# Where the stored queries and keys of two attention dilations are rotated: a GpSimd stream through DRAM, or VectorE one unit ahead

## The chip, the cores and the metric

The kernel runs on one core of one Trainium2 chip. A core has TensorE (PE, with a weight-load path PEld), VectorE (DVE), ScalarE (ACT), GpSimd (POOL) and SyncE (SP), each with an instruction queue of its own that is worked off in order. The metric is the device time of one execution in microseconds (us); less is better. In the profile `L126` is line 126 of the kernel, `psu<-t2h,w` is what an instruction writes and reads, and `[1.58 <-ACT u L365]` behind an instruction is the time its engine stood idle before it and what ended that.

## The reference

A decoder trunk of two layers over 1024 tokens of width 1024. Layer 0 mixes tokens with a gated delta rule and short convolutions, layer 1 with four HGRN2 heads (a gated recurrence) and with sliding-window attention in three dilations; each is followed by a dense feed-forward network. The change is in layer 1:

```python
SWA_PATTERNS = ((128, 1), (512, 4), (2048, 16))
...
def mixer_cd(h, w_in, lower_bound, norm_g, w_out):
    hq, hf, hi, hg, sq, sk, sv = split_cols(h @ w_in, CD_SPLITS)
...
    f_gate = lb + (1.0 - lb) * jax.nn.sigmoid(hf)
    o_c = hgrn2_recurrence(...)
...
    sq = rope(sq.reshape(b, t, n_pat, SWA_HEADS, SWA_DH), pos)
    sk = rope(sk.reshape(b, t, n_pat, SWA_HEADS, SWA_DH), pos)
...
def rope(x, pos):
    x1, x2 = xf[..., :half], xf[..., half:]
    return jnp.concatenate([x1 * cos - x2 * sin, x1 * sin + x2 * cos], axis=-1)
```

`rope` is the rotation: every head's 128 rows are two halves of 64; the result is the row times a cosine, plus the row of the other half times a signed sine. With the exchanged copy `x` of a tile `c` (its halves swapped) it is three element-wise instructions: `x*sin`, `c*cos`, and their sum.

## The kernel before

All large products are made in three passes of a reduced format (high by high, high by low, low by high), so `L126`, `L127`, `L128` are the three matmuls of one product, and `L102` and `L103` split a weight into its two parts on ACT and VectorE.

**The projection stage** (class `Pairs`) makes the queries and keys of dilation patterns 0 (dilation 1) and 2 (dilation 16), and the HGRN gates, with a product scheme that shares partial products between pairs of columns. For each pair, `pair` (L906) calls steps `p1` to `p7`. `p6` (L362) adds a product onto an accumulator `x[f]` and copies it to SBUF on ACT (L365, tile `u`); `p7` goes on adding onto the same accumulator, so PE must wait for that copy. Between `p6` and `p7` PE has the products of `p5`. `step` (L836) works off one piece of the forget gate of an HGRN head (`forget`, L816): among them a reciprocal on VectorE (L828), an instruction that makes `kk` from it (L830), and an activation on ACT that waits for it (L832). In this stage PE, VectorE, ACT, GpSimd, and from the pair loop on SyncE too, run in the order in which the code is written. The queries and keys go to DRAM unrotated, as `qk[p, h]` (L804).

**The mixer** (`mixer_cd`) then runs, on PE in the written order and on the other engines in the order that a scheduler picks by priority and readiness: the value projections of a dilation pattern (`swa_v`, whose tiles `sw` ACT copies at L1884 and SyncE writes to `scr_v` at L1885), the projection and VectorE rotation of pattern 1's queries and keys (`swa_qk`, L1914 and L1915), the HGRN recurrence (its level products at L1713 and L1715, its attention at L1791 and L1811, its norm at L1818 to L1825, of which L1821 is on GpSimd), and the attention itself. The attention has 12 units (`Attend`): pattern 1 heads 0 to 3, pattern 2 heads 0 to 3, pattern 0 heads 0 to 3. A unit has 4 steps of scores (PE L2014 and others from `k` and `q`, reduced by VectorE at L2020 or L2039), with flips and output products one and two steps later, and outputs that go out by SyncE as `scr_o<-ol` (L2090 and L2097).

The generator `local` gives one score step each time it is asked, and holds one unit ahead of the current one: `prepare` builds it, which issues its loads. A counter (`tick`) asks three generators as the projections go on: `local` at 0.7 and later 1.0 per unit of cost, the HGRN chain at 0.7, and the rotations at 0.5.

**The rotation stream** (`turns`) is that third generator. It has 32 items (two patterns, four heads, queries and keys, two halves). For each it loads a half `tc` (L1930) and its exchanged copy `tx` (L1931, L1932), rotates on GpSimd (L1943 for pattern 0, L1947 for pattern 2, the sum at L1948), and stores to DRAM as `fin` (L1950). A unit of patterns 2 and 0 reads `fin` when it is built:

```python
while not all((p, h, i, half) in turned for i in range(2) for half in range(NH)):
    next(turner)
self.q, self.k = tl("q", (2, HT), 2), tl("k", (2, HT), 2)
dma(self.k, final[p, h][1])
```

SyncE issues every one of these transfers, together with the weights (`raw`), the recurrence's loads (`f`, `kk`, `q` from `bkq`) and the value tiles.

## Time and profile before

| | before |
|---|---|
| median of 3 runs | 2625.44 us (2623.76 to 2626.53) |
| the profiled execution, its time | 2629.71 us |
| its span, first to last instruction | 2627.9 us |
| mean granted TensorE clock | 0.991 |
| DMA | 464.42 MB, mean 177 GB/s |

The rotation stream's part of GpSimd, from the groups of instructions between 1400 and 1600 us (line, engine, operation, tiles, shapes, count, then busy us, mean ns of one, and the engine's idle time before them with what ended it):

```profile
L1948 POOL TENSOR_TENSOR tc<-tc,tx 128x512 f32<-128x512 f32 x32 | 43.4, 1356 | 2.5
L1947 POOL TENSOR_TENSOR tc<-tc,turn 128x512 f32<-128x512 f32 x16 | 24.6, 1536 | 26.0 <-DMA tc<-qk 26.0
L1943 POOL TENSOR_TENSOR tc<-tc,turn 128x512 f32<-128x512 f32 x16 | 21.4, 1335 | 16.6 <-DMA tc<-qk 16.6
```

And its transfers on SyncE's queue (tiles, kind, count, size of one, median us from issue to landing):

```profile
tc<-qk SPq DMA_DIRECT2D x32, 256.0 KB, 3.8
fin<-tc SPq DMA_DIRECT2D x32, 256.0 KB, 3.8
k<-fin SPq DMA_DIRECT2D x8, 512.0 KB, 3.7
```

The stream is over by 1600 us: all 32 sums lie in that window, for units whose scores on PE begin at 1724.5 (pattern 2, L2032) and 1796.8 us (pattern 0).

### The profile page before, as it was taken

The numbers are of one execution on the slowest core, as the hardware profiler recorded it, in microseconds if no ns is written. First come the engines' busy times: TensorE is split into PE (matmuls) and PEld (weight loads), VectorE is DVE, ScalarE is ACT, GpSimd is POOL, SyncE is SP. The second block draws the span as 40 slices with busy tenths as digits, with TensorE's granted clock in tenths as the row PEclk, the third lists the DMA queues.
The fourth block names the chain that finished last, engine by engine and source line by source line (L and its number), as shares of the span: only waits on it lengthen the run. The fifth ranks groups of instructions, "written<-read, shape, count | busy, mean of one in ns | idle before, by whom it ended". The sixth has DMA issues, their size and how long they took to land.

```text
span 2627.9 us, 37803 instructions
## 1 busy us (share of the span) xinstructions
PE 2564.8 (98%) x14179; PEld 2138.1 (81%) x14179; DVE 1656.1 (63%) x2718; ACT 1032.6 (39%) x1855; POOL 643.5 (24%) x536
## 2 busy tenths in 40 slices
PE   8999999999999999999999879999999999999998
PEld 6888888888888888888788768878788888888887
DVE  7887776585656565566664675444667665566553
ACT  5432123343333344434343444455544333334442
POOL 1110111333333300133324762000024433331001
PEclk9999999999999999999999989999999999999999
DMA  4424346425556688533336874466662445668753
GB/s 141 137 98 163 108 150 216 145 85 168 188 185 220 206 300 285 182 112 124 117 111 222 258 212 138 113 169 214 191 237 74 164 166 197 206 204 288 268 186 119
DMA packets 291559, 464.42 MB, mean 177 GB/s; under 512 B 50704, under 2 KB 141616, under 8 KB 291248
## 3 DMA queue, kind: packets, MB, share of 16 engines
q1 hardware_dynamic: 291376, 462.01, 53.9%
q8 instruction: 111, 1.82, 0.3%
q14 instruction: 72, 0.59, 0.1%
HBM read 315.55 MB, written 146.36 MB: 176 GB/s over the span
## 4 chain that ended last, share of the span: by engine, by line
PE 79%; DVE 9%; DMA 4%; issue 3%; ACT 2%; POOL 2%; SPq 1%; POOLq 0%; DVEq 0%; ACTq 0%
PE psu L126 15%; PE psu L128 15%; PE psu L127 15%; PE psg L126 5%; PE psg L128 5%; PE psg L127 5%; PE psm L127 4%; PE psm L128 4%; PE psm L126 4%; DMA tc<-qk 1%; DVE fc L828 1%; DMA cm<-scr_o 1%; PE psm L2072 1%; DVE h L223 1%; DMA raw<-in_dram 1%
## 5 line engine op out<-in xcount | busy, mean ns | idle before, releaser
L103 DVE TENSOR_TENSOR w<-raw,w 128x1024 fp32r<-128x1024 f32 (+1 forms) x319 | 388.3, 1220 | 160.9 <-ACT w L102 160.4
L102 ACT CAST w<-raw 128x1024 fp32r<-128x1024 f32 (+1 forms) x319 | 306.8, 963 | 281.0 <-PE psu L128 134.7
L126 PE MATMUL psu<-hnh,w 128*128 128x512 f32 x888 | 356.8, 402 | 8.0 <-ACT w L102 8.0
L127 PE MATMUL psu<-hnl,w 128*128 128x512 f32 x888 | 349.1, 393 | 0.2 <-DVE hnl L2250 0.2
L128 PE MATMUL psu<-hnh,w 128*128 128x512 f32 x888 | 349.1, 393 | 0.0
L126 PEld LDWEIGHTS psu<-hnh,w 128*128 128x128 f32 x888 | 168.5, 190 | 42.2 <-ACT w L102 8.4
L128 PEld LDWEIGHTS psu<-hnh,w 128*128 128x128 f32 x888 | 168.3, 190 | 36.4 <-DVE w L103 0.8
L127 PEld LDWEIGHTS psu<-hnl,w 128*128 128x128 f32 x888 | 168.6, 190 | 34.2 <-DVE hnl L2250 0.8
L187 POOL TENSOR_TENSOR acc<-acc,sq 128x512 f32<-128x512 f32 x48 | 69.7, 1452 | 511.4 <-ACT sq L183 507.3
L302 POOL TENSOR_TENSOR ws<-raw 128x512 f32<-128x512 f32 x50 | 73.6, 1473 | 422.2 <-DMA raw<-in_dram 295.2
L103 DVE TENSOR_TENSOR w<-ws,w 128x1024 fp32r<-128x1024 f32 x47 | 61.6, 1311 | 116.0 <-ACT w L102 116.0
L103 DVE TENSOR_TENSOR hidq<-hr,hidq 128x1024 fp32r<-128x1024 f32 x72 | 82.2, 1143 | 73.8 <-ACT hidq L102 73.4
L102 ACT CAST hidq<-hr 128x1024 fp32r<-128x1024 f32 x72 | 70.2, 979 | 99.5 <-DMA hr<-ts 60.8
L126 PE MATMUL psm<-hidq,w 128*128 128x512 f32 (+1 forms) x275 | 106.1, 386 | 0.0
L128 PE MATMUL psm<-hidq,w 128*128 128x512 f32 (+1 forms) x275 | 105.9, 385 | 0.0
L127 PE MATMUL psm<-hidq,w 128*128 128x512 f32 (+1 forms) x275 | 105.9, 385 | 0.0
L126 PE MATMUL psu<-t3h,w 128*128 128x512 f32 x224 | 87.7, 392 | 5.6 <-ACT u L365 5.6
L393 POOL TENSOR_TENSOR hid<-hid,c 128x512 f32<-128x512 f32 x44 | 61.5, 1397 | 125.2 <-ACT hid L392 124.8
L308 POOL TENSOR_TENSOR raw<-raw,ws 128x512 f32<-128x512 f32 x47 | 61.3, 1304 | 121.0 <-DVE w L103 119.8
L126 PE MATMUL psu<-t4h,w 128*128 128x512 f32 x224 | 87.6, 391 | 0.6 <-ACT c L372 0.5
L127 PE MATMUL psu<-t3l,w 128*128 128x512 f32 x224 | 87.3, 390 | 0.0
L127 PE MATMUL psu<-t4l,w 128*128 128x512 f32 x224 | 87.3, 390 | 0.0
(489 smaller groups left out, 6655.2 us busy)
## 6 DMA issues: line engine op xcount, KB each, us to landing
raw<-in_dram SPq DMA_DIRECT2D x227, 512.0 KB, 3.7
sd<-in_dram SPq DMA_DIRECT2D x44, 512.0 KB, 3.7
hid<-hid SPq DMA_DIRECT2D x88, 256.0 KB, 3.1
sd<-sd SPq DMA_DIRECT2D x44, 512.0 KB, 3.3
hr<-ts SPq DMA_DIRECT2D x40, 512.0 KB, 4.9
raw<-sd SPq DMA_DIRECT2D x40, 512.0 KB, 4.0
hd<-h SPq DMA_DIRECT2D x48, 256.0 KB, 3.4
h<-hd SPq DMA_DIRECT2D x48, 256.0 KB, 5.8
```

Source lines behind the costliest of these rows:

```text
L102: S.copy(hi, src)
L103: eng.tensor_tensor(lo, src, hi.bitcast(F32), op=SUB)
L126: T.matmul(o, lh, rh, start=first and i == 0, stop=False, **kw)
L127: T.matmul(o, lh, rl, start=False, stop=False, **kw)
L128: T.matmul(o, ll, rh, start=False, stop=last and i == n - 1, **kw)
L187: (eng or G).tensor_tensor(a, a, q, op=ADD)
L223: V.scalar_tensor_tensor(h, h, vec[:, row + k:row + k + 1], pb, op0=MULT, op1=MULT)
L302: G.tensor_tensor(s[:, HT:], b[:, :HT], b[:, HT:], op=ADD)
L308: G.tensor_tensor(a[:, HT:], a[:, HT:], s[:, :HT], op=SUB)
L393: G.tensor_tensor(h, h, self.c22.pop(f), op=MULT)
L828: V.reciprocal(c, c)
L2072: T.matmul(po[:, jj * P:(jj + 1) * P], pt[:, z.start + i * P:z.start + (i + 1) * P], self.vp[:, j - m + 1 + i, :], start=i == 0, stop=i == ...
```

## The change

In `pair`, `p6` now stands ahead of the `step()` that stood ahead of it. The stream, its third counter, the tiles `tc` and `tx`, and the DRAM tensors `fin` are gone. A unit of patterns 2 and 0 loads its `k` and `q` unrotated from `qk`, and their exchanged copies as `rs` (two tiles of 512 KB, two buffers), when it is built; it leaves a list `todo` of four parts, each three VectorE instructions (two products and a sum, 128x512). `local` does two of the parts before the third and two before the fourth score step of the unit ahead of it, and what is left when the unit becomes the current one. The table of sines and cosines becomes one tile `turn` with room for the larger table; pattern 0's (1 MB) is loaded over the other's. Pattern 2's queries are rotated in place in their strided order.

```diff
@@ -931,8 +931,8 @@
             self.part_a(n, an)
             self.sums_late(an, bn, s)
             self.row1(f - 1, b22)
+            self.p6(f, t2)
             self.step()
-            self.p6(f, t2)
             self.p5(f, t1, psg())
             self.part_b(n, s)
             self.part_c(n, bn)
@@ -1893,13 +1893,22 @@
                     for tt, o in zip(tts, os_):
                         put(tt, o)
 
-            turn12 = tl("turn12", (2, 320))
-            dma(turn12, c_rope[:, :, T_LEN:])
-            final = {(p, h): dr.tile([2, P, 2, HT], F32, name=f"fin{p}{h}") for p in (2, 0) for h in range(4)}
+            table = {}
+
+            def turn(p):
+
+                if (p == 0) not in table:
+                    table.clear()
+                    t = table[p == 0] = tl("turn", (2, T_LEN))
+                    if p:
+                        dma(t[:, :, 0:320], c_rope[:, :, T_LEN:])
+                    else:
+                        dma(t, c_rope[:, :, 0:T_LEN])
+                return table[p == 0]
 
             def swa_qk(h, tick):
 
-                w = wload(("cd", 20 + h), ("cd", 32 + h))
+                w, turns = wload(("cd", 20 + h), ("cd", 32 + h)), turn(1)
                 qk = [tl("q", (2, HT), 2), tl("k", (2, HT), 2)]
                 for half in range(NH):
                     for i, z in enumerate(qk):
@@ -1911,44 +1920,10 @@
                         S.copy(x[64:128], o[0:64])
                         o3, x3 = (y.rearrange("p (i r) -> p i r", r=4) for y in (o, x))
                         for y, t in ((x3, 1), (o3, 0)):
-                            V.tensor_tensor(y, y, turn12[:, t, half * P:(half + 1) * P, None].to_broadcast([P, P, 4]), op=MULT)
+                            V.tensor_tensor(y, y, turns[:, t, half * P:(half + 1) * P, None].to_broadcast([P, P, 4]), op=MULT)
                         V.tensor_tensor(z[:, half].rearrange("p (r i) -> p i r", r=4), o3, x3, op=ADD)
                         tick(1)
                 return qk
-
-            def turns():
-
-                items = [(2, h, i, half) for h in range(4) for i in range(2) for half in range(NH)]
-                items += [(0, h, i, half) for half in range(NH) for h in range(4) for i in range(2)]
-                held, table, out = {}, {}, []
-
-                def ask_c(n):
-                    if n < len(items):
-                        p, h, i, half = items[n]
-                        held[n] = c, x = tl("tc", bufs=2), tl("tx", bufs=2)
-                        src = pairs.qk[p, h][i, :, half]
-                        dma(c, src)
-                        dma(x[0:64], src[64:128])
-                        dma(x[64:128], src[0:64])
-                ask_c(0)
-                for n, (p, h, i, half) in enumerate(items):
-                    if p == 0 and half not in table:
-                        table[half] = tl("turn0", (2, HT))
-                        dma(table[half], c_rope[:, :, half * HT:(half + 1) * HT])
-                        yield
-                    c, x = held.pop(n)
-                    ask_c(n + 1)
-                    for y, t in ((x, 1), (c, 0)):
-                        if p == 0:
-                            G.tensor_tensor(y, y, table[half][:, t], op=MULT)
-                        else:
-                            y3 = y.rearrange("p (r i) -> p r i", r=16)
-                            at = 256 + half * 32
-                            G.tensor_tensor(y3, y3, turn12[:, t, None, at:at + 32].to_broadcast([P, 16, 32]), op=MULT)
-                    G.tensor_tensor(c, c, x, op=ADD)
-                    yield
-                    dma(final[p, h][i, :, half], c)
-                    turned.add((p, h, i, half))
 
             def values(h, p):
                 vp = tl("vp", (8, P), 2)
@@ -1972,23 +1947,45 @@
 
                 def __init__(self, h, p, qk):
                     self.h, self.p = h, p
+                    self.todo = []
                     if p == 1:
                         self.q, self.k = qk
                     else:
-                        while not all((p, h, i, half) in turned for i in range(2) for half in range(NH)):
-                            next(turner)
-                        self.q, self.k = tl("q", (2, HT), 2), tl("k", (2, HT), 2)
-                        dma(self.k, final[p, h][1])
-                        if p == 2:
-                            c = self.q.rearrange("p b t -> p (b t)").rearrange("p (s b i) -> p b s i", s=16, b=2)
-                            for b in range(2):
-                                dma(c[:, b], final[p, h][0, :, b].rearrange("p (s i) -> p s i", s=16))
-                        else:
-                            dma(self.q, final[p, h][0])
+                        self.load(turn(p), pairs.qk[p, h])
                     self.vp = values(h, p)
                     self.tiles = [1 + ((p == 0 and j > 0) or (p == 1 and j % 2 == 1)) for j in range(8)]
                     self.sc, self.pt, self.po = {}, {}, None
                     self.st = tl("stat", (8, 2), 3)
+
+                def load(self, turns, src):
+
+                    self.k, self.q = tl("k", (2, HT), 2), tl("q", (2, HT), 2)
+
+                    def streams(ap):
+                        return ap.rearrange("p (s i) -> p s i", s=16) if self.p else ap
+
+                    def part(c, x, b):
+                        for y, t in ((x, 1), (c, 0)):
+                            if self.p:
+                                t = turns[:, t, None, 256 + b * 32:288 + b * 32].to_broadcast([P, 16, 32])
+                            else:
+                                t = turns[:, t, b * HT:(b + 1) * HT]
+                            V.tensor_tensor(y, y, t, op=MULT)
+                        V.tensor_tensor(c, c, x, op=ADD)
+
+                    for i, t in ((1, self.k), (0, self.q)):
+                        if self.p and i == 0:
+                            c4 = t.rearrange("p b t -> p (b t)").rearrange("p (s b i) -> p b s i", s=16, b=2)
+                            cs = [c4[:, b] for b in range(2)]
+                            for b in range(2):
+                                dma(cs[b], src[i, :, b].rearrange("p (s i) -> p s i", s=16))
+                        else:
+                            cs = [streams(t[:, b]) for b in range(2)]
+                            dma(t, src[i])
+                        x = tl("rs", (2, HT), 2)
+                        dma(x[0:64], src[i, 64:128])
+                        dma(x[64:128], src[i, 0:64])
+                        self.todo += [lambda c=cs[b], y=streams(x[:, b]), b=b: part(c, y, b) for b in range(2)]
 
                 def blocks(self, n):
 
@@ -2151,7 +2148,7 @@
                 end[1]()
 
             lead = {}, {}, {}, (6, 7)
-            ready, late, diag, turned, holding, combined = [], [], [], set(), [0], [0]
+            ready, late, diag, holding, combined = [], [], [], [0], [0]
 
             def local():
 
@@ -2164,7 +2161,13 @@
                 while True:
                     nxt = None
                     prepare()
+                    if now and ahead and now[1] > 1:
+                        for turn_part in ahead[0].todo[:2]:
+                            turn_part()
+                        del ahead[0].todo[:2]
                     if not now and ahead:
+                        for turn_part in ahead[0].todo:
+                            turn_part()
                         now += [ahead.pop(), 0]
                         prepare()
                     holding[0] = len(ahead) + bool(now)
@@ -2185,13 +2188,13 @@
                     yield
 
             busy = [False]
-            hg_chain, loc, turner = chain(), local(), turns()
-            works = (loc, hg_chain, turner)
-            due, rate = [0.0] * 3, [0.0, 0.7, 0.5]
+            hg_chain, loc = chain(), local()
+            works = (loc, hg_chain)
+            due, rate = [0.0] * 2, [0.0, 0.7]
 
             def tick(cost):
 
-                for i in range(3):
+                for i in range(2):
                     due[i] += cost * rate[i]
                 while max(due) >= 1:
                     for i, work in enumerate(works):
```

**SyncE while the value tiles of pattern 2 are projected.** The rows of an engine's order give line, operation, and tiles (`scr_v` value tiles to DRAM, `raw` a weight, `kk` and `q<-bkq` inputs of the recurrence, `vt` its values). SyncE before, at the start of this stretch:

```order
L1931 DMA tx<-qk_9313 64x512
L1932 DMA tx<-qk_9313 64x512
L115 DMA raw<-in_dram 128x1024
L1930 DMA tc<-qk_9313 128x512
L1885 DMA scr_v_11037<-sw 128x512
L1950 DMA fin_11054<-tc 128x512
L1885 DMA scr_v_11037<-sw 128x512
L1931 DMA tx<-qk_9314 64x512
L1932 DMA tx<-qk_9314 64x512
L1885 DMA scr_v_11037<-sw 128x512
L1930 DMA tc<-qk_9314 128x512
L1950 DMA fin_11054<-tc 128x512
```

SyncE of the changed kernel at the same place:

```order
L115 DMA raw<-in_dram 128x1024 x2
L1762 DMA vt<-scr_h 128x4x128
L1694 DMA kk<-bkq_9318 128x512
L1694 DMA q<-bkq_9318 128x512
L1885 DMA scr_v_11037<-sw 128x512 x4
L1762 DMA vt<-scr_h 128x4x128
```

The value tiles, which stood between loads and stores of the rotation, now follow one another.

**ACT in `pair`.** In the order of ACT before, the activation of the forget gate (L832) and then the copy of `p6` (`u`); `w` are weight casts and `d` is another accumulator's copy:

```order
L832 ACTIVATE fc<-fc,lb,omlb 128x512
L338 COPY gt<-psu 128x512
L857 COPY d<-psu 128x32x16
L102 CAST w<-raw 128x1024
L832 ACTIVATE fc<-fc,lb,omlb 128x512
L365 COPY u_10138<-psu 128x512
L102 CAST w<-ws 128x1024
```

and of the change:

```order
L832 ACTIVATE fc<-fc,lb,omlb 128x512
L338 COPY gt<-psu 128x512
L857 COPY d<-psu 128x32x16
L102 CAST w<-raw 128x1024
L365 COPY u_10132<-psu 128x512
L832 ACTIVATE fc<-fc,lb,omlb 128x512
L102 CAST w<-ws 128x1024
```

The copy has moved ahead of the second activation.

**SyncE at the handover from pattern 2 to pattern 0.** Before: `k` and `q` of the first unit of pattern 0 from `fin`, among output tiles `scr_o<-ol` and value tiles:

```order
L2097 DMA scr_o<-ol 64x4x130 x2
L1981 DMA k<-fin_11057 128x1024
L1987 DMA q<-fin_11057 128x1024
L2097 DMA scr_o<-ol 64x4x130 x2
L115 DMA raw<-in_dram 128x1024 x3
L2097 DMA scr_o<-ol 64x4x130 x2
L1885 DMA scr_v_11036<-sw 128x512 x2
```

The change, at the same place (the first two `rs` are the exchanged halves of the keys, the others of the queries; line 2094 was line 2097):

```order
L115 DMA raw<-in_dram 128x1024
L1984 DMA k<-qk_9309 128x1024
L1986 DMA rs<-qk_9309 64x1024
L1987 DMA rs<-qk_9309 64x1024
L2094 DMA scr_o<-ol 64x4x130 x2
L1885 DMA scr_v_11036<-sw 128x512
L1984 DMA q<-qk_9309 128x1024
L1885 DMA scr_v_11036<-sw 128x512
L1986 DMA rs<-qk_9309 64x1024
L2094 DMA scr_o<-ol 64x4x130 x2
L1885 DMA scr_v_11036<-sw 128x512
L1987 DMA rs<-qk_9309 64x1024
```

The queries and their exchanged halves now stand behind two output tiles and three value tiles of the running unit. VectorE at that place in the change (`q`, `rs` as above, `k` the next unit's keys; L2017 is the score reduction of pattern 0, which was L2020; `ol<-stat` belongs to the outputs, `ss` and `e` to the recurrence's norm):

```order
L1973 TENSOR_TENSOR q<-q,turn 128x512 x2
L2089 COPY ol<-stat 64x4x2
L2091 COPY ol<-stat 64x2x2 x2
L1819 TENSOR_SCALAR ss<-ss 128x4
L1825 TENSOR_TENSOR e_15325<-psg,rr 128x512
L1973 TENSOR_TENSOR rs<-rs,turn 128x512 x2
L1974 TENSOR_TENSOR q<-q,rs 128x512 x2
L1973 TENSOR_TENSOR k<-k,turn 128x512 x2
L2017 ISA sc,stat<-psm,cf 128x128
```

The rows of L1973 and L1974 are new here. The sums of the queries (L1974) now stand just ahead of the first score reduction of pattern 0, with two products of the next unit's keys between.

## The prediction

> **What bounds the kernel now.** I read the busy times first, then the chain that ended last, the stretches of the stage that the change touches, and the waits of TensorE (PE) in them.
>
> ```profile
> PE 2564.8 (98%) x14179; PEld 2138.1 (81%) x14179; DVE 1656.1 (63%) x2718; ACT 1032.6 (39%) x1855; POOL 643.5 (24%) x536
> ...
> PE 79%; DVE 9%; DMA 4%; issue 3%; ACT 2%; POOL 2%; SPq 1%; POOLq 0%; DVEq 0%; ACTq 0%
> ```
>
> PE is busy for 98% of the span and its instruction order is the same in both kernels, row for row. So a gain can only come out of PE's idle time and out of the time at a lowered clock, and a loss is a new PE wait. The profiled execution took 2629.7 us, with a span of 2627.9 us; the median of the three runs is 2625.4 us, 4.3 below it. I sum against the 2629.7 and put the sum on the median. The next view has stretches of layer 1's mixer; its columns are the stretch, its length, then busy time (and count) of PE, PE's weight loads, VectorE (DVE), ScalarE (ACT), GpSimd (POOL), then the granted clock, the DMA share and GB/s.
>
> ```profile
> 1400.00:1500.00 100.00, 90.80 (x900) 78.59 (x900) 53.04 (x81) 36.58 (x95) 69.38 (x51) 0.95 0.76 241
> 1500.00:1600.00 100.00, 85.18 (x923) 75.92 (x922) 71.14 (x127) 45.02 (x125) 66.53 (x49) 0.93 0.72 217
> 1600.00:1700.00 100.00, 97.38 (x903) 82.09 (x902) 58.08 (x153) 49.02 (x137) 2.09 (x2) 0.98 0.41 109
> ```
>
> POOL works for two thirds of the first two stretches, and these hold the PE's idle time: 9.2 + 14.8 = 24.0 us, against 2.6 us in the third, where the rotations are done. The PE's waits between 1400 and 1600 (engine, line, what it waited for: total us, times, longest) give the same 24:
>
> ```profile
> PE psm L2014 <- DVE k L1915: 12.2, 1, 12.2
> PE psg L1811 <- ACT attn L1791: 7.4, 2, 6.8
> PE psm L2061 <- ACT sc L2021: 2.2, 2, 2.0
> PE psg L1814 <- DVE st L1807: 1.8, 2, 1.4
> PE psm L2014 <- DVE stat L2020: 0.5, 1, 0.5
> ```
>
> No row names GpSimd, so I follow each wait one step back.
>
> ```profile
> 1448.73 0.58 ACT L1884 COPY sw<-psu 128x512 f32<-128x512 f32 x1 [9.09 <-DMA scr_v<-sw]
> ...
> 1558.22 0.69 DVE L1825 TENSOR_TENSOR e<-psg,rr 128x512 f32<-128x512 f32 x1 [3.47 <-POOL rr L1821]
> ...
> SPq L1950 <- POOL tc L1948: 44.5, 24, 4.6
> ...
> L1713 DVE TENSOR_TENSOR kd<-kd,dd 128x256 f32<-128x256 f32 x18 | 19.3, 1073 | 0.9 <-ACT e L1818 0.5
> ...
> L1713 DVE TENSOR_TENSOR kd<-kd,dd 128x256 f32<-128x256 f32 x18 | 7.6, 424 | 1.7 <-ACT m L1710 1.1
> ```
>
> Three ways lead back to the stream. SyncE issues every transfer in order and stood 44.5 us behind rotated tiles (third row); so ACT, ahead of the attention tile, stood 9.09 us for a value tile's write (first row). DVE stood 3.47 us for `rr`, which is queued on GpSimd behind the rotations (second row). And the same VectorE instruction takes 1073 ns between 1410 and 1560 but 424 ns between 1600 and 1720 (last two rows): beside the GpSimd stream VectorE is 2.5 times as slow. The Trainium skill, "SBUF — State Buffer", section "Who interferes with whom", says that VectorE and GpSimd share one port pair under an exclusive lock; the two means agree, and by that rule this slowing goes with the stream. I count it only where it ends as PE idle time, which the 24 us already hold.
>
> **(a) `p6` ahead of `step()`: -5.6 us.** The PE waits between 1150 and 1400, then PE and ACT around one of four like places:
>
> ```profile
> PE psu L126 <- ACT u L365: 5.6, 4, 1.6
> ...
> 1265.03 0.39 PE L128 MATMUL psu<-t2h,w 128*128 128x512 f32 x1
> ...
> 1268.38 0.81 ACT L832 ACTIVATE fc<-fc,lb,omlb 128x512 f32<-128x512 f32 x1 [6.26 <-DVE kk L830]
> 1269.10 0.56 ACT L365 COPY u<-psu 128x512 f32<-128x512 f32 x1
> ```
>
> `p6` is complete at 1265.4, but its copy starts at 1269.10, because the forget gate's activation stands ahead of it on ACT and waits 6.26 us for VectorE. With the copy first it runs at about 1265.5, under the 2.7 us of `p5` matmuls that follow on PE, and `p7` finds it done. What is late next is the activation, 0.56 us later at most; its readers are weight casts and gate pieces of the next pair. I count the four waits whole; bounds: -5.6 to -3.
>
> **(b) The stream is taken out: -18.8 us.** Gone are 96 GpSimd instructions, 32 stores and their reads, 44.5 us of SyncE's standing. If 1400 to 1600 then ran as 1600 to 1700 does, 2 x 2.6 = 5.2 us of the 24.0 would stay: -18.8. Bounds: all gone, -24; or only the 12.2 and the 6.8 halve because the forget-gate recurrence, which feeds both, has waits of its own, -9.5.
>
> **(c) The clock after the long waits: -5.1 us.**
>
> ```profile
> 1453.70:1459.30 5.60, 5.56 (x20) 5.09 (x21) 3.01 (x6) 2.72 (x12) 4.15 (x4) 0.51 0.93 297
> 1563.70:1568.50 4.80, 4.77 (x20) 4.59 (x21) 0.64 (x4) 1.58 (x5) 4.64 (x5) 0.51 0.52 151
> 1629.20:1634.10 4.90, 4.86 (x14) 3.91 (x15) 0.64 (x4) 0.99 (x4) 0.00 (x0) 0.65 0.38 107
> ```
>
> Behind the 6.8 and the 12.2 us wait the PE ran at 0.51 for 5.6 and 4.8 us, which cost (5.6 + 4.8) x 0.49 = 5.1. Where the waits go, that goes: 0 to -5.1. The third row, behind a wait of 2.2 us that I leave in place, lost 4.9 x 0.35 = 1.7.
>
> **(d) 96 rotations on VectorE, of which the first 60 here: +1 us.** VectorE's own rotations of the second pattern have this form already:
>
> ```profile
> 1654.17 0.69 DVE L1914 TENSOR_TENSOR sw<-sw,turn 128x512 f32<-128x512 f32 x1 [0.77 <-ACT sw L1911]
> 1654.78 0.69 DVE L1914 TENSOR_TENSOR psu<-psu,turn 128x512 f32<-128x512 f32 x1
> ...
> 1658.71 0.69 DVE L1825 TENSOR_TENSOR e<-psg,rr 128x512 f32<-128x512 f32 x1 [1.14 <-POOL rr L1821]
> 1661.81 0.69 DVE L1914 TENSOR_TENSOR sw<-sw,turn 128x512 f32<-128x512 f32 x1 [1.95 <-ACT sw L1911]
> ...
> 1664.36 0.47 PE L126 MATMUL psu<-w,hnh 128*128 128x512 f32 x1 [0.41 <-DVE k L1915]
> ...
> L1915 DVE TENSOR_TENSOR q<-psu,sw 128x512 f32<-128x512 f32 x4 | 4.3, 1074 | 0.0
> ...
> 1420.41 2.00 DVE L103 TENSOR_TENSOR w<-raw,w 128x1024 fp32r<-128x1024 f32 x1 [13.19 <-ACT w L102]
> ...
> 1666.60:1796.80 130.20, 127.76 (x1365) 105.90 (x1365) 52.80 (x220) 69.18 (x229) 2.76 (x3) 1.00 0.58 158
> ```
>
> From start to start one takes 0.61 us, so 96 take 58.6 us (103 at the 1.07 of the strided sum). I take 0.61, since new sums read and write plain rows, but for the queries of dilation 16. Each unit has 12, or 7.3 us. The first unit's four products of exchanged copies fall near the 13.19 us in which VectorE stood for a weight. Its other eight, 4.9 us, stand in the order among the last rotations of pattern 1's head 3 (1654 to 1663), where VectorE's idle times are 0.77, 1.14 and 1.95, 3.86 in all: 1.0 too little, and PE already waits 0.41 us for the last sum there. So +1.0, from 0 to +3. From 1666.6 to 1796.8 the 48 of four units take 29.3 of 77 idle us: 0 (PE waits 2.4 us there now); were the cover gone, 29.3 would be the price.
>
> **(e) The handover from dilation 16 to dilation 1: +7.9 us.** This is the one new wait that the order shows. The queries of the first dilation-1 unit are rotated only when both exchanged halves have landed, and SyncE issues these in between output and value tiles:
>
> ```profile
> 1785.87 0.58 ACT L2078 COPY ol<-psm 128x512 f32<-128x512 f32 x1
> 1786.48 1.25 SPq L2097 DMA_DIRECT2D scr_o<-ol  x2
> ...
> 1794.20 1.25 SPq L2097 DMA_DIRECT2D scr_o<-ol  x2
> 1795.55 0.55 SPq L1885 DMA_DIRECT2D scr_v<-sw  x1
> 1796.80 0.82 PE L2014 MATMUL psm<-k,q 128*128 128x128 f32 x4
> ...
> tx<-qk SPq DMA_DIRECT2D x64, 128.0 KB, 3.7
> ```
>
> The second half of the copies stands right behind the value tile of 1795.55, so it goes out at about 1796.1. With the 3.7 us of such a transfer it lands at 1799.8, and four VectorE instructions (4 x 0.61 = 2.4) end at 1802.2, against PE's need at 1796.80: a wait of 5.4. Behind it I put half a clock as in (c), 5.1 x 0.49 = 2.5 us: +7.9. Queued behind the waiting instruction on VectorE are the next unit's first products and the score reductions, on which PE waits anyway. Bounds: 0, if SyncE runs ahead because nothing stands on rotated tiles any more, to +11 with the next unit's products in between. The Trainium skill, "TensorE: Matmul & The Clock Gate", section "What's actually happening", has the clock halved after an idle window of about 3.4 us and released after one busy window; by that the clock would cost an estimated 1.7 here in place of 2.5. The 0.65 behind a wait of only 2.2 us speaks against reading that threshold strictly, and I keep the rows.
>
> **(f) The dilation-1 units: +2 us.** The stages of the four units:
>
> ```profile
> 1796.80:1815.30 18.50, 18.50 (x104) 15.95 (x103) 8.19 (x40) 9.23 (x28) 0.26 (x1) 1.00 0.69 209
> 1815.30:1835.40 20.10, 20.10 (x119) 17.55 (x118) 12.87 (x62) 8.63 (x28) 0.00 (x0) 1.00 0.74 225
> 1835.40:1857.00 21.60, 21.18 (x118) 17.35 (x117) 13.62 (x57) 12.21 (x36) 0.00 (x0) 1.00 0.68 217
> ```
>
> With 7.3 us more VectorE needs 15.5 of 18.5, 20.2 of 20.1 and 20.9 of 21.6 us. The work fits, barely, but bursts of two parts (six instructions, 3.7 us) stand ahead of score reductions that PE waits for: I take +2, from 0 to +12 (a burst uncovered in each unit). The exchanged copies add 1 MB a unit at a DMA share of 0.7, instead of the rotated stream's traffic; 0 to +3, within the same bound.
>
> **Sum:** -5.6 - 18.8 - 5.1 + 1.0 + 7.9 + 2 = -18.6, so 2611.1 for an execution like the profiled one, and 2625.4 - 18.6 = **2606.8 us** at the median's level.
>
> **The rivals.**
> *R1, the waits go and nothing new comes.* VectorE's idle time takes all rotations and SyncE, freed of 44.5 us, issues the handover's copies early: (a), (b) at -24, (c), and (d), (e), (f) at 0: -34.7, or 2591. For it speaks that in 1600 to 1700 PE already runs at 97%; against it, the order at the handover.
> *R2, the waits only change their names.* The 12.2 us wait ends on VectorE, and the recurrence that feeds PE there has the same number of steps after the change; half of (b) and (c) stays: -5.6 - 9.5 - 2.5 + 10.9 = -6.7, or 2619. For it speaks that all five waits name ACT or VectorE; against it, 1073 ns against 424.
> *R3, slower.* VectorE, in order, becomes the bound of the dilation-1 stages: each burst of 3.7 us holds a score group of PE. It decides as soon as a burst is not covered by VectorE's idle time before it; two bursts in each of the eight rotated units are 16 x 3.7 = 59 us, of which the slack of the dilation-16 units (77 us idle) takes about half: +29.5, with +7.9 from (e), +1.0 from (d) and -29.5 from (a) to (c): +8.9, or 2634. Against it speaks that VectorE is 41% busy (52.8 of 130.2 us) in dilation 16.
> *R4, the stream was hidden.* Then the idle time of 1400 to 1600 has to do with the stage and not with GpSimd, and (a) alone acts, less (d) and (e): +3.3, or 2629.
>
> **How the numbers follow.** Forecast 0.60, R1 0.17, R2 0.14, R3 0.06, R4 0.03. This kernel's measurement can tell 0.2%, 5.25 us, from no change. The forecast and R1 lie below 2620.2, R2 in two of three cases: faster 0.86; R4 and the rest of R2: same 0.08; R3: slower 0.06. The forecast's own bounds, (a) and (b) at their ends with (e) and (f), are 2595 to 2618; with R1 and most of R2 the range is 2591 to 2620.
>
> **What would show it.** (a): no PE wait on L365 between 1150 and 1400. (b): POOL nearly empty, PE at 97 and L1713 at 424 ns in 1400 to 1600. (c): clock 0.98 or more there. (d): products at 0.61 from start to start, and PE's wait on the last sum of pattern 1 under 3 us. (e): one PE wait of 5 us on VectorE's query sum at the first dilation-1 scores, with half clock behind it. (f): DVE at 97% in the second dilation-1 stage, PE waits there of 2 us in all. I am wrong if a PE wait of 6 us or more stays in the old stretch, or if the rotations hold PE in several units.

## The result, and the profile after

| | before | after |
|---|---|---|
| median of 4 runs each | 2625.99 us (2623.76 to 2628.83) | 2601.91 us (2600.62 to 2604.10) |
| ratio of the runs | | 0.9909, 95% interval 0.9891 to 0.9926 |
| profiled execution, its time and span | 2629.71, 2627.9 us | 2600.88, 2599.1 us |

The kernel is 24.1 us faster (0.9%). The forecast was 18.6 us faster, 2606.8 us. Of all executions behind this document one, of `p6_alone`, was slow (6072.59 us), and no ratio counts it. First the busy times, then the stretches of the mixer in the changed kernel (length, busy time of PE, PEld, DVE, ACT, POOL, granted clock, DMA share, GB/s), which answer to those of before:

```profile
PE 2555.1 (98%) x14179; PEld 2129.6 (82%) x14179; DVE 1662.7 (64%) x2814; ACT 1033.5 (40%) x1855; POOL 514.4 (20%) x440
...
1400.00:1500.00 100.00, 100.00 (x1051) 85.59 (x1051) 46.17 (x107) 43.27 (x106) 2.02 (x2) 1.00 0.43 128
1500.00:1600.00 100.00, 97.64 (x1088) 86.81 (x1086) 55.68 (x145) 51.99 (x148) 2.01 (x2) 1.00 0.33 99
...
1700.00:1800.00 100.00, 90.71 (x756) 74.93 (x756) 69.84 (x236) 48.21 (x168) 2.02 (x2) 0.97 0.83 206
```

Between 1400 and 1600 us PE's idle time has fallen from 24.0 to 2.4 us, and VectorE is busy for 102 us there against 124, though four rotation products were added: its level products take 421 ns in place of 1073. The last stretch shows the price: PE has 9.3 us of idle time in 1700 to 1800.

Stretches at the same microsecond hold different work once one kernel is ahead. Since the order on PE is the same in both, the same instruction can be looked up in each instead. The next rows (line, engine, instruction, count, duration of one, then first and last start) are, for before and then for after: the reciprocals of the forget gates, all scores of pattern 2, all scores of pattern 0.

```profile
L828 DVE RECIPROCAL fc<-fc x8: 3320/3336/3344, 1254.8 to 1383.5; 128x512 f32<-128x512 f32 x8
L2032 PE MATMUL psm<-k,q x128: 221/222/271, 1724.5 to 1791.5; 128*64 128x64 f32 x128
L2014 PE MATMUL psm<-k,q x64: 272/379/484, 1796.8 to 1878.9; 128*128 128x256 f32 x56, 128*128 128x128 f32 x8
...
L828 DVE RECIPROCAL fc<-fc x8: 3320/3332/3342, 1252.3 to 1375.8; 128x512 f32<-128x512 f32 x8
L2029 PE MATMUL psm<-k,q x128: 222/222/270, 1689.9 to 1756.8; 128*64 128x64 f32 x128
L2011 PE MATMUL psm<-k,q x64: 272/378/634, 1768.9 to 1851.8; 128*128 128x256 f32 x56, 128*128 128x128 f32 x8
```

The differences of these starts give the time of each stage, before and after. The last column is the experiment `no_rotation`, below.

| stage | before | after | change | no_rotation |
|---|---|---|---|---|
| start to first reciprocal (untouched) | 1254.8 | 1252.3 | -2.5 | 1255.1 |
| first to last reciprocal (`p6`) | 128.7 | 123.5 | -5.2 | 123.5 |
| to the first score of pattern 2 | 341.0 | 314.1 | -26.9 | 309.1 |
| to the first score of pattern 0 | 72.3 | 79.0 | +6.7 | 72.4 |
| to the last score of pattern 0 | 82.1 | 82.9 | +0.8 | 78.3 |
| to the end | 749.0 | 747.3 | -1.7 | 748.0 |

Of the 28.8 us between the two profiled executions, 24.6 lie in the four changed stages; 4.2 lie in work that the change doesn't touch and are the difference of two executions.

### The profile page after: what moved, and what is told of

Read it like the earlier page. It is cut to its first block, busy times and chain, and to the rows that moved or that the text cites. A ratio compares the mean times of both kernels' runs of the same rounds, so it can differ in the third digit from the quotient of the medians.

```text
span 2599.1 us, 37598 instructions
## 1 busy us (share of the span) xinstructions
PE 2555.1 (98%) x14179; PEld 2129.6 (82%) x14179; DVE 1662.7 (64%) x2814; ACT 1033.5 (40%) x1855; POOL 514.4 (20%) x440
## 5 line engine op out<-in xcount | busy, mean ns | idle before, releaser
L103 DVE TENSOR_TENSOR w<-raw,w 128x1024 fp32r<-128x1024 f32 (+1 forms) x319 | 381.5, 1198 | 155.8 <-ACT w L102 155.0
L103 DVE TENSOR_TENSOR hidq<-hr,hidq 128x1024 fp32r<-128x1024 f32 x72 | 82.1, 1141 | 76.0 <-ACT hidq L102 75.5
L126 PE MATMUL psu<-t3h,w 128*128 128x512 f32 x224 | 87.3, 390 | 1.0 <-ACT u L365 1.0
L126 PE MATMUL psu<-t4h,w 128*128 128x512 f32 x224 | 87.5, 391 | 0.5 <-ACT c L372 0.5
L128 PE MATMUL psu<-t4h,w 128*128 128x512 f32 x224 | 87.2, 389 | 0.0
L128 PE MATMUL psu<-t3h,w 128*128 128x512 f32 x224 | 87.1, 389 | 0.0
```

Of the source, the lines that this page charges most:

```text
L103: eng.tensor_tensor(lo, src, hi.bitcast(F32), op=SUB)
L126: T.matmul(o, lh, rh, start=first and i == 0, stop=False, **kw)
L128: T.matmul(o, ll, rh, start=False, stop=last and i == n - 1, **kw)
```

## The experiments

**`p6` alone, and the rotations left out.** `p6_alone` is the kernel before with the two lines of `pair` exchanged. `no_rotation` is the changed kernel with this edit:

```diff
-                            V.tensor_tensor(y, y, t, op=MULT)
-                        V.tensor_tensor(c, c, x, op=ADD)
+                            pass
```

> The kernel before with p6 ahead of step() and nothing else. If the copy of p6 was held by the forget gate's activation, the waits of PE on L365 between 1150 and 1400 us fall from 5.6 us to 1.0 us at most, PE's idle time from 1400 to 1600 us stays at 24 us, and the time is 5 us below before (2621). If the activation or the weight casts behind the copy become late in turn, the waits return under another name and the time is that of before within 1.5 us.

> The changed kernel with the 96 VectorE rotation instructions of dilations 16 and 1 left out and all their loads kept (the exchanged copies are loaded and read by nothing). If the rotations are hidden in VectorE's idle time but for the handover, the time falls by the handover's VectorE part and the wait for the exchanged halves, 6 to 10 us, and every other stage keeps its length within 2 us. If the rotations hold score groups in the dilation-1 stages, these get shorter too, and the time falls by 12 us or more. If the queries' own load is as late as the exchanged halves, a wait of 2 us or more stays at the handover.

`p6_alone` took 2618.45 us against 2624.24 (ratio 0.9977, 0.9967 to 0.9986): 5.8 us less. Its wait of PE between 1150 and 1400 us, by engine and line waited for, total, times and longest:

```profile
PE psu L126 <- ACT u L365: 1.0, 1, 1.0
```

Three of the four waits are gone, one of 1.0 us stays, and none came in their place. PE's idle time in 1400 to 1600 us, which was to stay at 24, is 21.1 us here; the stream is the same, so that two executions of it can differ by 3 us there. `no_rotation` took 2588.32 us against 2622.73 (0.9865, 0.9847 to 0.9883). That is 13.6 us below the changed kernel, or 11.6 by the two ratios to before, about the 12 that was set for "rotations hold other stages too". Its rows for the table above:

```profile
L828 DVE RECIPROCAL fc<-fc x8: 3323/3334/3339, 1255.1 to 1378.6; 128x512 f32<-128x512 f32 x8
L2028 PE MATMUL psm<-k,q x128: 222/222/270, 1687.7 to 1754.8; 128*64 128x64 f32 x128
L2010 PE MATMUL psm<-k,q x64: 272/378/483, 1760.1 to 1838.4; 128*128 128x256 f32 x56, 128*128 128x128 f32 x8
```

So the 96 instructions cost 5.0 us before pattern 2's first score, 6.6 up to the handover, and 4.6 behind it, 16.2 in all (the two executions differ by less, since the untouched start of `no_rotation` was 2.8 us longer). The loads, which it keeps, make no wait at the handover by themselves: 72.4 us is the length of before.

**Which hold of the GpSimd stream cost the 24 us?** The prediction named three ways back to it: VectorE slowed beside GpSimd (A in the expectations), SyncE standing behind rotated tiles (B), and `rr` queued on GpSimd (C). `stream_idle` leaves out the stream's `G.tensor_tensor` lines and keeps its transfers.

> The kernel before with the 96 GpSimd instructions of the stream left out, all its loads and stores kept (the queries and keys of dilations 1 and 16 stay unrotated). If GpSimd beside VectorE is what costs, L1713 falls from 1073 to about 424 ns, the 12.2 us wait on L1915 goes, and the time falls by 20 to 29 us. If SyncE's standing behind the stream's stores and loads is what costs, L1713 also falls, but the 6.8 us wait for the attention copies stays and the time falls by 12 to 15 us only. If the bytes are what costs, nothing changes by more than 3 us.

2601.94 us against 2624.24 (0.9914, 0.9896 to 0.9932): 22.3 us less, with all of the stream's bytes still moved. Its two stretches, and the level product that took 1073 ns:

```profile
1400.00:1500.00 100.00, 96.28 (x923) 82.83 (x922) 37.40 (x96) 40.19 (x103) 2.02 (x2) 0.98 0.82 265
1500.00:1600.00 100.00, 97.85 (x1125) 86.74 (x1124) 57.07 (x147) 51.09 (x143) 2.02 (x2) 1.00 0.70 218
...
L1713 DVE TENSOR_TENSOR kd<-kd,dd 128x256 f32<-128x256 f32 x21 | 8.9, 422 | 2.2 <-ACT m L1710 1.5
```

PE's idle time is 5.9 us at a DMA share of 0.70 to 0.82. What cost was GpSimd's work, not the bytes. The signs of the first theory are all there, but the run does not show it alone: with GpSimd's work all three holds go. To part A from B, `in_pieces` cuts each GpSimd instruction in four, as in

```diff
-                    G.tensor_tensor(c, c, x, op=ADD)
+                    for z in range(0, HT, P):
+                        G.tensor_tensor(c[:, z:z + P], c[:, z:z + P], x[:, z:z + P], op=ADD)
```

> The kernel before, with each of the stream's 96 GpSimd instructions cut into four of 128x128 (same elements, same transfers, same order). Two theories of the lost 24 us. A, VectorE stands for the whole of a GpSimd instruction that runs when it starts: with pieces of about 0.4 us L1713 falls from 1073 to some 450 to 600 ns, and at least half of PE's idle time of 24 us in 1400 to 1600 us goes: 8 to 15 us faster than before. B, SyncE stands for rotated tiles: GpSimd needs as long for a tile as before or longer (1.6 us in place of 1.35), SyncE stands as long, and the time is that of before within 4 us.

2644.44 us, 21.7 *above* before (1.0079, 1.0060 to 1.0097). Both times missed, though A's 450 to 600 ns held, and the rows say how (level products; then waits in 1400 to 1600 us of SyncE, of VectorE and of PE):

```profile
L1713 DVE TENSOR_TENSOR kd<-kd,dd 128x256 f32<-128x256 f32 x18 | 9.2, 510 | 2.1 <-ACT m L1710 1.3 <-DVE dd L1715 0.5
...
SPq L1953 <- POOL tc L1951: 66.8, 24, 4.9
...
DVE e L1825 <- POOL rr L1821: 23.0, 3, 16.9
...
PE psm L2017 <- DVE k L1915: 17.2, 1, 17.2
PE psg L1811 <- ACT attn L1791: 11.3, 1, 11.3
```

VectorE's slowing was more than halved (1073 to 510 ns, 424 alone) and the kernel became slower. GpSimd needed longer for a tile, SyncE stood 66.8 in place of 44.5 us, `rr` came 16.9 us late once, and the old two waits of PE grew. So B and C grew while A shrank, and the time says nothing on what A cost before.

`rr_on_vector` takes C away: at L1821, `V.reciprocal(rr, ss)` in place of GpSimd's instruction.

> The kernel before, with the recurrence's rr (L1821) made on VectorE by a reciprocal in place of GpSimd's reciprocal root (its values differ; the instruction count and the rest are the same). Theory C: VectorE's waits for rr, queued on GpSimd behind the rotations, are what leads on to PE's 24 us: then these go, and the time falls by 8 us or more. If SyncE's standing behind rotated tiles (B) or the lock between VectorE and GpSimd (A) leads there, the 7.8 us of waits for rr go, but PE's idle time in 1400 to 1600 us stays above 16 us and the time is 0 to 6 us below before.

2619.13 us against 2623.59 (0.9979, 0.9967 to 0.9992): 4.5 us less, as its second theory expected. The longest wait of PE in 1400 to 1600 us, 12.2 us before, is now

```profile
PE psm L2014 <- DVE k L1915: 8.2, 1, 8.2
```

20.9 us of PE's idle time stay, so C is the smaller part, at this length of the queue. How large it can get, `gpsimd_only` shows. It was meant to add GpSimd's work to the changed kernel without a transfer (the tile's fill and the third counter are left out here):

```diff
+                gx = tl("gx", (256,))
...
+                for n in range(32):
+                    for i in range(6):
+                        G.tensor_tensor(gx, gx, gx, op=MULT)
+                    yield
```

> The changed kernel with a third generator at the old rate of 0.5 that issues 192 GpSimd products of 128x256 on one tile of its own (half the elements of one old instruction, twice the count), which nothing reads; no transfer is added. If GpSimd slows VectorE, L1713 rises from 421 ns to 800 ns or more while these run, and PE waits on VectorE's sums come back: 8 to 20 us slower than the changed kernel. If the cost was SyncE's standing, the time is that of the changed kernel within 3 us.

2658.07 us, 56 us above the changed kernel, outside both expectations. With no transfer to pace it, GpSimd had 148 of these instructions in its queue when `rr` came (GpSimd, then VectorE):

```profile
1392.04 108.98 POOL L2196 TENSOR_TENSOR gx<-gx 128x256 f32<-128x256 f32 x148
...
1502.02 0.69 DVE L1825 TENSOR_TENSOR e<-psg,rr 128x512 f32<-128x512 f32 x1 [55.31 <-POOL rr L1821]
```

It tells nothing on A, since C swamped it. For B, `own_queue` has GpSimd issue the stream's own transfers (`G.dma_start` for `dma`), and `own_queue_rr` takes C away from it as well.

> The kernel before, with the stream's 128 loads and stores issued by GpSimd itself instead of SyncE; its rotations stay as they are. B, SyncE stands for rotated tiles: SyncE's 44.5 and 23.0 us of waits at L1950 and L1930 go, PE's waits in 1400 to 1600 us go with them, and the time falls by 18 to 25 us. A, VectorE stands for GpSimd: L1713 stays at about 1050 ns and at least two thirds of the 24 us stay; 0 to 8 us faster. If GpSimd's issuing delays rr (L1821) further, the wait of VectorE at L1825 grows past 3.5 us and the time may be that of before or above it.

> The kernel of own_queue (the stream's loads and stores issued by GpSimd) with rr made on VectorE as in rr_on_vector. SyncE and rr are both free of the stream, and only the slowing of VectorE beside GpSimd (A) and the bytes are left. If A costs, L1713 stays near 1 us and PE's idle time in 1400 to 1600 us stays above 12 us: 0 to 12 us faster than before. If A is hidden and GpSimd's queue with SyncE's is the whole cause, PE's idle time there falls under 8 us and the time is 16 to 24 us below before, against 55 us above it in own_queue.

`own_queue` took 2678.26 us (1.0207, 1.0189 to 1.0226) and `own_queue_rr` 2649.49 (1.0094, 1.0063 to 1.0125); by their times both theories miss. In `own_queue` VectorE's waits for `rr` grew to 36.8 us. In `own_queue_rr` one transfer of the stream had stayed on SyncE, the second half of pattern 0's table, whose tile GpSimd still read. The two stretches, the level product in the first of them, SyncE's wait for that table in 1400 to 1600 us and the table's issue, then the two longest waits of PE and a wait of ACT in the second stretch:

```profile
1400.00:1500.00 100.00, 97.98 (x1012) 84.23 (x1012) 61.35 (x98) 41.80 (x104) 73.75 (x82) 1.00 0.72 222
1500.00:1600.00 100.00, 62.34 (x610) 54.75 (x600) 67.70 (x98) 30.52 (x87) 88.31 (x101) 0.79 0.57 179
...
L1713 DVE TENSOR_TENSOR kd<-kd,dd 128x256 f32<-128x256 f32 x15 | 10.5, 699 | 1.4 <-ACT m L1710 1.0
...
SPq L1937 <- POOL tc L1943: 61.3, 1, 61.3
...
1576.16 0.56 SPq L1937 DMA_DIRECT2D turn<-in_dram  x1
...
1559.95 1.22 PE L2014 MATMUL psm<-k,q 128*128 128x256 f32 x2 [15.71 <-DVE k L1915]
...
1589.89 0.37 ACT L1699 COPY sw<-psu 128x256 f32<-128x256 f32 x1 [22.72 <-DMA scr_h<-sw]
...
1591.09 1.18 PE L2061 MATMUL psm<-cf,sc 128*128 128x128 f32 x3 [15.14 <-ACT sc L2021]
```

In the first 100 us GpSimd works for 73.75 and VectorE's products are slowed to 699 ns, but nothing of the stream stands in SyncE's queue: PE is busy for 97.98 us, against 90.80 before, and the old wait of 6.8 us is gone. In the second PE loses 38 us, in two ways. The wait of 15.14 us is SyncE's (B): it stands at the table for 61.3 us, until 1576.16, ACT stands 22.72 us for a write to `scr_h` that SyncE issues only behind it, at 1579.92, and PE stands for ACT. The wait of 15.71 us ends on VectorE's sum `k`, and SyncE has no part in it, as the five rows further down show.

**What the two long waits of the kernel before hang on.** The wait of 6.8 us first. ACT has copied its second value tile, SyncE issues a rotated tile, and only then the first value tile's write:

```profile
1437.30 0.59 ACT L1884 COPY sw<-psu 128x512 f32<-128x512 f32 x1 [0.77 <-PE psu L128]
...
1441.02 0.32 SPq L1950 DMA_DIRECT2D fin<-tc  x1
...
1443.73 0.38 SPq L1885 DMA_DIRECT2D scr_v<-sw  x1
```

The 9.09 us of ACT that the prediction shows are its wait for such a write to land, and PE's 6.8 us follow. In the first stretch of `own_queue_rr`, with SyncE free of the stream and VectorE still slowed, this wait does not occur; in `rr_on_vector` it is 7.2 us long. So it is B.

The wait of 12.2 us ends on VectorE's sum `k` (L1915). From the copy of the recurrence's state (L1805) to that sum VectorE has the same instructions in each run, with the reciprocal as one more where it was put there. This stretch in before, `rr_on_vector`, `in_pieces`, `own_queue_rr` and `stream_idle` (length, busy time of PE, PEld, DVE, ACT, POOL, clock, DMA share, GB/s):

```profile
1536.30:1563.70 27.40, 15.24 (x97) 13.45 (x95) 23.52 (x34) 10.31 (x31) 18.43 (x14) 0.84 0.61 180
1537.15:1560.90 23.75, 15.57 (x98) 13.69 (x96) 23.26 (x34) 10.42 (x31) 15.90 (x12) 0.91 0.61 177
1552.16:1584.95 32.79, 15.57 (x98) 13.69 (x96) 15.41 (x33) 9.70 (x29) 25.28 (x52) 0.78 0.52 161
1528.67:1559.95 31.28, 15.57 (x99) 13.69 (x97) 30.77 (x34) 10.57 (x32) 30.28 (x33) 0.82 0.34 116
1525.33:1541.45 16.12, 15.57 (x98) 13.69 (x96) 13.37 (x33) 9.48 (x29) 1.01 (x1) 1.00 0.75 211
```

VectorE (the third busy time) needs 13.4 us for this work when GpSimd rotates nothing, and 23.5 beside the stream. In the kernel before it stands only once in it, 3.47 us for `rr`, and never for a transfer. In `rr_on_vector` it does not stand at all, and PE still waits 8.2 us: that is A. In `in_pieces` its work is down to 15.4 us, and 16.9 us are its wait for `rr`: C. In `own_queue_rr` 30.8 of 31.3 us are work: A again, and stronger, with GpSimd's issues beside its rotations.

So of the 24.0 us, 6.8 hang on SyncE (B), 8 to 9 on VectorE's slowing (A), and 3.5 on `rr` (C; 1.1 at this place in `p6_alone`). The other 5 us are shorter waits for ACT and VectorE that no run takes apart. A run that removes A alone was not made; its share is read from the rows above.

**The engine or the way through DRAM?** `stream_on_vector` keeps the stream and its transfers, but writes `V.tensor_tensor` for `G.tensor_tensor`, and has `p6` ahead.

> The kernel before with p6 ahead of step() and the stream's 96 rotation instructions on VectorE instead of GpSimd; its loads and stores through DRAM stay. If the engine was the cause and not the way through DRAM, PE's idle time in 1400 to 1600 us falls from 24 to 8 us or less and there is no wait at the handover: 2593 to 2603, at or below the changed kernel. If VectorE, which works in order, stands for the stream's tiles as GpSimd did, for 20 us or more, new PE waits on VectorE show in 1400 to 1640 us and the time is 2605 to 2625.

2607.99 us against 2623.59 (0.9936, 0.9918 to 0.9954), within the times of the second theory, at their lower end. SyncE's waits in 1400 to 1600 us:

```profile
SPq L1930 <- DMA fin<-tc: 32.2, 22, 3.9
...
SPq L1950 <- DVE tc L1948: 9.6, 11, 1.9
```

SyncE's standing for rotated tiles falls from 44.5 to 9.6 us, and PE's idle time in 1400 to 1600 us to 15.3, above the 8 of the first theory. But the loads still stand 32.2 us for the stores of the tile that they overwrite, and VectorE, in order, waits 28.8 us for the stream's tiles. Of the 15.6 us gained here 5.8 are `p6`'s, so 9.8 come from the engine with the way through DRAM kept. Ending that way looks worth some 6 us on top (2607.99 against 2601.91), with the handover's wait already paid, but the intervals of the two ratios overlap.

**Can the handover's wait be had back?** Three versions of the changed kernel move loads up. `loads_first` wraps `self.load(...)` in `tc.high_priority()` for all units, `handover` for the first unit of pattern 0 only; `rs_first_half` does it for that unit's exchanged copies only and loads half of its table early.

> The changed kernel with a higher priority for the loads of a unit of dilations 16 and 1, so that the exchanged halves of the first dilation-1 unit are issued ahead of the output and value tiles of the running one. If the late issue of the last exchanged half holds the handover, the 6.6 us wait at the first dilation-1 scores falls under 1.5 us and its half clock goes: 6 to 9 us less than the changed kernel, about 2594. If the DMA engines, which were 0.99 busy there, are the bound, the wait stays at 4 us or more. If keys and queries, whose buffers come free late, are now last, the wait is 2 to 4 us. Loads that stand for buffers at the head of SyncE's queue could hold the value tiles: then a new PE wait of 3 us or more shows between 1640 and 1770 us.

> The changed kernel with a higher priority for the loads of the first dilation-1 unit alone, the table included; in loads_first all units had it, and its gain at the handover was lost to a wait of 6.1 us for value tiles. If the late exchanged half alone costs the 6.6 us and the half clock behind it, the handover's wait falls under 2 us and the time by 5 to 9 us below the changed kernel, about 2594 to 2597. If loads that stand for a buffer at the head of SyncE's queue hold output tiles, value tiles or weights, a new wait of 4 us or more shows on PE between 1735 and 1775 us and the time is that of the changed kernel within 3 us.

> The changed kernel with a higher priority for the exchanged copies of the first dilation-1 unit alone, and half of its table loaded early into a tile of its own, so that 512 KB less are moved at the handover; keys and queries keep their place. If the late exchanged halves and the 1 MB of the table made the 6.6 us wait, it falls under 2.5 us and the time is 3 to 8 us below the changed kernel (2594 to 2599). If what is moved ahead pushes back the output and value tiles as in handover, a wait of 3 us or more shows elsewhere between 1740 and 1860 us, and the time is that of the changed kernel within 3 us.

They took 2604.22, 2607.15 and 2606.27 us (ratios to before 0.9924, 0.9930, 0.9924; the changed kernel's is 0.9909): no gain. PE's waits in 1600 to 1880 us, the largest of each in this order:

```profile
PE psu L126 <- ACT sw L1884: 6.1, 1, 6.1
...
PE psu L2132 <- DVE ol L2125: 5.2, 1, 5.2
...
PE psu L2132 <- DVE ol L2125: 8.8, 4, 4.7
```

The 6.6 us wait is gone in two of them; in `rs_first_half` 2.9 us of it stay, above the 2.5 that were expected. In `loads_first` a wait of 6.1 us for value tiles came instead; in the profiled execution of `handover`, the longest of its five, pattern 0's scores take 94.2 us (1765.8 to 1860.0) in place of 82.9. Which of the transfers pushed back costs this was not tried. None of the versions that compute the whole is faster than the changed kernel.

## Why the prediction was right, and where its sizes were off

The mechanism and the sign were right, and the time lies in the range. That the number came within 6 us is in part luck: against the stages of the two traces the terms are off by +0.4 (a), -8.0 (b and c), +4.0 (d), +0.9 (e) and -3.4 (f), which cancel to -6.

- **(a) `p6`, -5.6:** measured -5.2 in the traces and -5.8 by `p6_alone`. One of the four waits, which were counted whole, stayed at 1.0 us.
- **(b) and (c), -23.9 together:** `no_rotation` shows them without (d): 341.0 to 309.1 us, -31.9, of which 23.9 are idle time and 8.0 the clock. The term that (b) had mis-sized is the 5.2 us of idle time that it left in place because 1600 to 1700 had it: the work that had 24.0 us of waits kept 0.6. In (c) only the clock behind the two longest waits was counted; the low clock behind the wait at 1629 us, 1.7 us, went too, though a wait of 1.8 us stays at that place.
- The three ways back that the prediction gave for (b) all carry time, and so does what it held against R2: the 1073 against 424 ns are most of the 12.2 us wait, with `rr`, and SyncE's standing is the 6.8 us one.
- **(d), +1.0:** +5.0. PE's wait for the last sum of pattern 1 came as foretold, but longer, and a low clock behind it was not counted. The wait in the changed kernel and the stretch behind it:

```profile
1627.22 0.77 PE L126 MATMUL psu<-w,hnh 128*128 128x512 f32 x1 [2.95 <-DVE k L1924]
...
1628.00:1634.00 6.00, 6.00 (x143) 4.76 (x143) 1.69 (x8) 1.93 (x8) 0.00 (x0) 0.56 0.55 164
```

  2.95 us against 0.41, and 6 x 0.44 = 2.6 at the lowered clock: 5.1. The clock was counted behind the new wait of (e), and not behind this one.
- **(e), +7.9:** 6.64 us of wait and 5.1 x 0.43 = 2.2 of clock, 8.8. The chain is the forecast one: SyncE issues the last exchanged half, VectorE waits for it, PE for VectorE, and then the stretch at the low clock.

```profile
1761.52 0.48 SPq L1987 DMA_DIRECT2D rs<-qk  x1
...
1766.94 1.29 DVE L1973 TENSOR_TENSOR rs<-rs,turn 128x512 f32<-128x512 f32 x2 [3.12 <-DMA rs<-qk]
1768.15 1.29 DVE L1974 TENSOR_TENSOR q<-q,rs 128x512 f32<-128x512 f32 x2
...
1768.94 1.62 PE L2011 MATMUL psm<-k,q 128*128 128x128 f32 x4 [6.64 <-issue]
...
1768.90:1774.00 5.10, 5.06 (x17) 4.29 (x18) 3.33 (x11) 0.99 (x4) 0.00 (x0) 0.57 1.06 211
```

  The half landed 5.4 us after its issue instead of 3.7, at a DMA share of 0.99 (1762.3 to 1768.9 us). PE's row says "issue": the profile matched no releaser to this wait. The first of VectorE's two query sums, 0.69 us long, ends at 1768.84, 0.1 us before PE goes on, and `no_rotation` has no such wait; that shows whose it is.
- **(f), +2:** pattern 0's stage, without the 2.2 us of clock that belong to (e), is 82.9 - 2.2 = 80.7 us. Against the 78.3 without rotations that is +2.4, the size that was forecast. Against the 82.1 of before, from which the sum went, it is -1.4. The last of the four units, which the prediction did not show, ran at a lowered clock before, behind a wait of 3.3 us:

```profile
1857.00:1878.90 21.90, 18.56 (x89) 15.70 (x88) 15.74 (x65) 12.82 (x36) 0.00 (x0) 0.84 0.63 187
```

  That cost 21.9 x 0.16 = 3.5 us. In the changed kernel and in `no_rotation` this wait is 1.2 and 2.6 us long and the clock behind it 1.00; why was not tried. It is a gain that the forecast did not have.
- **The rivals.** R1 (nothing new comes) falls with (d) and (e). R2 falls: the 12.2 us wait is gone, and nothing of its size came in its place between 1400 and 1600 us. R3 falls: the rotations hold PE at two places and not in each unit. R4 falls with `stream_idle`.

## What to carry to other kernels

A stream of work that nobody waits for by name can still set the pace, through the queue that issues everybody's transfers, through an engine that it slows, and through a short instruction that stands behind it. Which of these costs is a question to each wait, not to the stage: here the two longest waits, 110 us apart, had different causes. Follow each back to the last engine that worked without a stop or stood. An experiment that cuts one hold and lengthens another, as smaller pieces did, cannot rank them by its time; the busy time of one engine over the same instructions, in run after run, can. A wait that is taken out at an engine's queue can reappear where the new work needs its transfers latest; count a lowered clock behind each new wait, the short ones too.

## What the runs showed of the hardware

VectorE's level product took longer the longer the GpSimd instructions beside it were: 424 ns alone, 1073 on average beside instructions of 1.3 to 1.5 us, 510 beside pieces of 0.5 us. The Trainium skill, "SBUF — State Buffer", section "Terms", says that the lock on their shared ports is held for the full instruction and that the loser fully blocks; these three means agree. In `own_queue_rr`, where GpSimd also issues transfers, one product of 0.69 us (L1914) took 4.14, from 1552.59 us, while two GpSimd instructions of 1.27 and 1.28 us and two issues ran to their end; what else held it is not shown. Between 1500 and 1560 us of that run the five such products on `sw`, a tile in SBUF, took 2670 ns on average, while the five on `psu`, an accumulator in PSUM, kept their 686. Whether the slowing costs time depends on what PE waits for: some 8 us at the 12.2 us wait, and next to nothing in the first stretch of `own_queue_rr`, where PE was busy for 97.98 of 100 us.

GpSimd pays for being cut: the four pieces of a sum in `in_pieces` (L1951), of 496 ns each, are 1.98 us, against 1356 ns for the whole sum.

And the clock fell to 0.56 for 6 us behind a PE wait of only 2.95 us, nearly as far as behind 6.64 us (0.57 for 5.1 us). It stayed at 1.00 behind a wait of 1.77 us in the same kernel (1591.1 to 1596.0 us) and behind one of 2.56 us in `no_rotation` (1828.5 to 1838.4 us), but fell to 0.65 behind the 2.22 us that the prediction shows. The prediction cited an idle window of about 3.4 us from the Trainium skill, "TensorE: Matmul & The Clock Gate", section "What's actually happening"; shorter waits were enough here, and the length of the wait alone does not tell which.
